# Sums of weights at a fixed place, more buffers, and block copies on another engine, in a hybrid decoder layer on one core

## Chip, cores and metric

The kernel runs on one core of a Trainium2 chip. The metric is the device time of one execution in microseconds (us). The engines are called TensorE (PE in the profile), VectorE (DVE), ScalarE (ACT), GpSimd (POOL) and SyncE (SP), which here issues nearly all transfers.

## What is computed

One decoder layer on 16 learned meta tokens and 1024 tokens of width 1024, all in float32: a SwiGLU FFN added at half weight, a token mixer added, a second FFN at half weight, a final norm.

```python
def swiglu(x, w_in, w_out):
    gate, up = jnp.split(x @ w_in, 2, axis=-1)
    return (jax.nn.silu(gate) * up) @ w_out

h = jnp.concatenate([meta, x], axis=1)
h = h + 0.5 * swiglu(rms_norm(h, ffn1_norm), ffn1_w_in, ffn1_w_out)
h = h + hybrid_mixer(rms_norm(h, mix_norm), ...)
h = h + 0.5 * swiglu(rms_norm(h, ffn2_norm), ffn2_w_in, ffn2_w_out)
return rms_norm(h, final_norm)[:, N_META:]
```

The mixer projects to 10256 columns and runs two branches of eight heads each: a gated DeltaNet (a causal convolution, then per chunk a triangular system and a scan over a 128x128 state) and a retention (rotary, a causal product with decay, a scan). Their outputs are gated, projected and added. The decay between two tokens of a chunk is used only where the second is not earlier than the first (the causal mask, `incl`).

## The kernel before

**Products.** Every float32 weight tile of 128x512 is loaded raw (`wraw`), cast on ScalarE to its rounded part (`wh`, `L136`) and split on GpSimd or VectorE into the rest (`wl`, `L137`); a product is three matmuls (`mm3`, `L158` to `L160`). `wraw`, `wh` and `wl` have four buffers each (`wtile`).

**The FFN** (`ffn`, called twice; tiles are named `start` in the first and `ffn` in the second) works on the 2816 hidden columns in 22 blocks `f` of 128. Each block makes Strassen-like combinations: `pair_weights` (`L220` to `L231`) takes four raw tiles (two of the gate, two of the up weights), adds and subtracts them in place on VectorE (`L223`, `L224`, `L226`, `L227`) and yields seven weight combinations in the order 0, 1, 2, 3, 5, 4, 6. `hidden` multiplies each with two groups of tokens; the list `order` has 14 entries `(i, grp)`. Products 0, 2, 4, 6 of a group grow in one PSUM bank (`mm`), 1 in a `px` bank and 3, 5 in another; between them ScalarE copies and VectorE's `add` (`L295`) reads the bank, so product 6 cannot start before the `add` that reads product 4. Gates are multiplied at `L298`; blocks with f % 4 of 0 or 1 also subtract at `L301`, those of 2 or 3 combine with the stored halves of block f - 2 in a tile `kept` (`L289` to `L312`). Finished operands go to DRAM (`opnd_d`).

After five groups of four blocks, `output` multiplies the operands with combinations of `w_out`. Those that need additions are made ahead in the hidden loop: at f = 4, 8, ..., 20 `load_sums` (`L378`) loads four 256 KB parts twice into tiles `sums`, and at f % 4 == 1, or at f = 20 for the last two, `weight_sums` (`L384`) does four VectorE additions of 128x512 (`L386` to `L389`) on each and stores 1 MB to `sums_d` (`L390`). The ten tiles per FFN, `kept`, the operand halves (`lower`, `upper`), `opnd`, `hh` and `hl` share the tag `hid` with two buffers.

**The mixer.** Retention runs first, a projection and a scan per head; after the projections of heads 1 to 4 `decays` makes the decay matrices of two DeltaNet heads each: a product on GpSimd (`L981`), a matmul, an exponential on ScalarE (`L986`), a store to `em_d`. Then `weave` interleaves the DeltaNet's chains with the remaining projections on TensorE, head by head. `gdn_systems` scales the key products by the decay into `X` (`L1125`), copies its 32x32 diagonal blocks to `Xc` on VectorE (`L1129`, four copies), goes through DRAM (`x_d`) for a substitution within blocks of 16 (`L1159`, `L1160`), doubles the inverses and copies blocks of 32 from `Uc` to `Ut` (`L1201`, four copies), then multiplies blocks (`tmp` at `L1213`, `L1218`). `gdn_scan` makes `Qk` (`L1287`), masks it with `incl` on GpSimd (`L1291`) and runs the state recurrence (`L1302` to `L1314`, state `st` at `L1312`).

**Order.** Each engine works through its own queue in order, SyncE's transfers too. The program's order is only a priority: the framework's planner runs a simulation of time (`schedule_with_timeline_sim`) and puts an instruction into its engine's queue when the simulated engine is free and its data and buffer are there. So an instruction can stand in a queue well ahead of its place in the program.

Of the kernel before, what the change touches and what calls it, by code (L numbers as in the profile page):

```python
# [10 lines left out]
F32 = mybir.dt.float32  # L11
F32R = mybir.dt.float32r
AF = mybir.ActivationFunctionType
ALU = mybir.AluOpType
PSUM = bass.MemoryType.PSUM

P = 128
# [79 lines left out]
def hybrid_layer(ctx, tc, a):  # L97
    nc = tc.nc
# [39 lines left out]
        return hi, lo  # L138

    def wtile(tag):  # L140
        return wp.tile([P, 4, P], F32 if tag == "wraw" else F32R, name=tag, tag=tag, bufs=4)

    def load_half(src):
        raw = wtile("wraw")
# [86 lines left out]
        yield 6, put_weights(rg[1], eng=V if 6 in fast else None)  # L231

    def operand_halves(fp, hn):
        return halves_of([fp.tile([P, 8 * hn], F32, name=n, tag="hid", bufs=2) for n in ("lower", "upper")])

    def halves_of(ts):
        return [t.rearrange("p (k h n) -> p k h n", k=4, h=2)[:, :, h] for h in range(2) for t in ts]
# [37 lines left out]
    def ffn(fp, hidp, hT, hn, slots, spare, second, w_in, w_out, last_blocks, last_weights, tail, first, w0=None):  # L275
# [6 lines left out]
        def hidden(f, ws, order, after):  # L282
            sg, q3, q1, q2 = (fp.tile([P, 2, hn], F32, name=n, tag="tmp", bufs=5) for n in ("sg", "q3", "q1", "q2"))
            chains = [[None, None], [None, None]]
            made = [0, 0]
            kept = None
            if f and f % 4 == 0:
                sums.extend(load_sums(f // 2 - 2 + e) for e in range(2))
            if f < 4 * ng and f % 4 > 1:  # L289
                kept = hidp.tile([P, 8 * hn], F32, name="kept", tag="hid", bufs=2).rearrange("p (u n) -> p u n", u=4)  # L290
                for u, i in enumerate((0, 4)):
                    SP.dma_start(kept[:, u], part_of(f - 2, i))

            def add(out, ps):
                V.tensor_tensor(out=out, in0=out, in1=ps, op=ALU.add)  # L295

            def gate(half, grp, x, g):
                V.tensor_tensor(out=x[:, grp], in0=x[:, grp], in1=g[:, grp], op=ALU.mult)  # L298
                made[half] += 1
                if half and f < 4 * ng and f % 4 < 2:  # L300
                    V.tensor_tensor(out=x[:, grp], in0=x[:, grp], in1=q3[:, grp], op=ALU.subtract)  # L301
                if made[half] == 2:
                    put_hidden(f, half, x)
                    if half and kept is not None:
                        flat = lambda t: t.rearrange("p g n -> p (g n)")
                        b11, t1, t2, d = (kept[:, u] for u in range(4))
                        V.tensor_tensor(out=t2, in0=flat(q2), in1=t1, op=ALU.subtract)
                        SP.dma_start(part_of(f, 2), t2)
                        G.tensor_tensor(out=b11, in0=t2, in1=b11, op=ALU.subtract)
                        SP.dma_start(part_of(f, 3), b11)  # L310
                        G.tensor_tensor(out=d, in0=flat(q3), in1=t2, op=ALU.subtract)
                        SP.dma_start(part_of(f, 5), d)  # L312

            for i, grp in order:
                if grp == 0 and sums and (f % 4 == 1 and i in (2, 5) or f == 4 * ng and i in (5, 6)):
                    weight_sums(*sums.pop(0))
                chain = i in (1, 3, 5)
                if i in (0, 1, 3):
                    chains[chain][grp] = psum(("mm", "px")[chain])[:, :hn]
                ps = chains[chain][grp]  # L320
                (wh, wl), (xh, xl) = ws[i], slots[grp][i]
                mm3(ps, [(wh[:, k], wl[:, k], xh[:, k], xl[:, k]) for k in range(4)], i in (0, 1, 3), i in (1, 5, 6), True)
                if i == 0:
                    S.copy(sg[:, grp], ps)
                elif i == 1:
                    add(sg[:, grp], ps)
                    S.activation(sg[:, grp], sg[:, grp], AF.Silu)
                elif i == 2:
                    S.copy(q3[:, grp], ps)
                elif i == 3:  # L330
                    S.copy(q2[:, grp], ps)
                elif i == 5:
                    add(q3[:, grp], ps)
                    gate(0, grp, q3, sg)
                elif i == 4:
                    add(q2[:, grp], ps)
                else:
                    S.activation(q1[:, grp], ps, AF.Silu)  # L338
                    gate(1, grp, q2, q1)
                if grp == 0:  # L340
                    after(i)
# [34 lines left out]
        sums = []  # L376

        def load_sums(n):  # L378
            w = hidp.tile([P, 8 * hn], F32, name="sums", tag="hid", bufs=2)[:, :16 * P].rearrange("p (i c) -> p i c", i=4)
            for i, (dh, fi) in enumerate(((0, 0), (0, 1), (1, 0), (1, 1))):  # L380
                SP.dma_start(w[:, i].rearrange("p (f c) -> p f c", f=2), block(4 * (n // 2), n % 2, fi, dh))
            return n, w

        def weight_sums(n, w):  # L384
            a11, a12, a21, a22 = (w[:, i] for i in range(4))
            V.tensor_tensor(out=a21, in0=a21, in1=a22, op=ALU.add)  # L386
            V.tensor_tensor(out=a11, in0=a21, in1=a11, op=ALU.subtract)
            V.tensor_tensor(out=a12, in0=a12, in1=a11, op=ALU.subtract)
            V.tensor_tensor(out=a22, in0=a22, in1=a11, op=ALU.subtract)  # L389
            SP.dma_start(sums_d[n], w.rearrange("p i c -> p (i c)"))  # L390

        LOADS = ((0, 1), (2, 3), (5, 4), (6,))

        def load_operands(g, pair):
            t = hidp.tile([P, 8 * hn], F32, name="opnd", tag="hid", bufs=2).rearrange("p (u k n) -> p u k n", u=2, k=4)
            for u, i in enumerate(pair):
                SP.dma_start(t[:, u].rearrange("p k n -> p (k n)"), opnd_d[7 * g + i])
            return t
# [65 lines left out]
            for _ in steps:  # L464
                pass
        f0 = 4 * ng
        hh, hl = (hidp.tile([P, 8 * hn], F32R, name=n, tag="hid", bufs=2) for n in ("hh", "hl"))
        for q in range(4):
            s = slice(2 * hn * q, 2 * hn * q + 2 * hn)
            raw = fp.tile([P, 2, hn], F32, name="raw", tag="tmp", bufs=5).rearrange("p a n -> p (a n)")  # L470
# [497 lines left out]
    def decays(hs):  # L968
# [9 lines left out]
        for h in hs:  # L978
            for gi, g in enumerate(GROUPS):
# [4 lines left out]
                ef = em.rearrange("p c d -> p (c d)")  # L984
                PE.matmul(pd, lhsT=strict, rhs=ef, start=True, stop=True)
                S.activation(ef, pd, AF.Exp)  # L986
                SP.dma_start(em_d[h][gi], ef)

    for h in range(H):
# [104 lines left out]
    def gdn_systems(h, kraw, vraw):  # L1094
# [31 lines left out]
                                       in1=ems[c // 4][:, c % 4], op0=ALU.mult, op1=ALU.mult)  # L1126
        for q in range(4):
            qs = slice(B2 * q, B2 * q + B2)
            V.tensor_copy(Xc[qs], X[qs, :, qs])  # L1129
        V.tensor_scalar(x16[:, :NCH], Xc[:, :, 0:BS], par[:, 0:1], None, op0=ALU.mult)  # L1130
        V.scalar_tensor_tensor(out=x16[:, :NCH], in0=Xc[:, :, BS:B2], scalar=par[:, 1:2], in1=x16[:, :NCH], op0=ALU.mult, op1=ALU.add)
        V.tensor_scalar(xoff[:, :, BS:B2], Xc[:, :, BS:B2], par[:, 0:1], None, op0=ALU.mult)
# [65 lines left out]
        tmp = bp.tile([P, CK * BS * BS * 3 // 4], F32, name="tmp", tag="xr", bufs=1)  # L1198
        for q in range(4):
            qs = slice(B2 * q, B2 * q + B2)  # L1200
            V.tensor_copy(Ut[qs, :, qs], Uc[qs])  # L1201

        At = tmp[:, :512].rearrange("p (c x) -> p c x", x=64)
        ps = psum("px")
# [40 lines left out]
    def gdn_scan(h, query, kf, vf, st, Ut, ems, rk, br, kd_s, v_s):  # L1245
# [33 lines left out]
        for j in range(0, NCH, 2):  # L1279
# [5 lines left out]
            for i in range(2):  # L1285
                c = j + i
                V.scalar_tensor_tensor(out=Qk[:, c], in0=ps[:, i * P:(i + 1) * P], scalar=rk[:, c + 1:c + 2],  # L1287
                                       in1=ems[c // 4][:, c % 4], op0=ALU.mult, op1=ALU.mult)
            if j % 4 == 2:
                qg = Qk[:, j - 2:j + 2]  # L1290
                G.tensor_tensor(out=qg, in0=qg, in1=incl.unsqueeze(1).broadcast_to([P, 4, P]), op=ALU.mult)  # L1291


        sso = sp.tile([P, CK], F32, name="sso")
# [259 lines left out]
```

## Time and profile before

| | us |
|---|---|
| median of 3 runs | 3125.59 |
| lowest and highest | 3121.34, 3128.95 |
| profiled execution | 3128.13 |
| its span, first to last instruction | 3126.2 |
| mean granted TensorE clock | 0.966 of full |

The profile comes from the profiled execution. A line of it names engine, kernel line, operation, the tile written and, behind the arrow, those read. A busy share is the time in which the engine executed; a wait names the engine and instruction that ended it. The granted clock is a share of 2.4 GHz and takes two levels, 2.4 and 1.2 GHz, so a mean of 0.93 is 14% of a stretch at the lower one. The stages in order: start and FFN1 to about 710 us, retention to 1316, DeltaNet with projections to 2090, branch outputs to 2400, FFN2 to the end.

### The profile page before, as it was taken

The numbers are of one execution on the slowest core, as the hardware profiler recorded it, in microseconds if no ns is written. First come the engines' busy times: TensorE is split into PE (matmuls) and PEld (weight loads), VectorE is DVE, ScalarE is ACT, GpSimd is POOL, SyncE is SP. The second block draws the span as 40 slices with busy tenths as digits, with TensorE's granted clock in tenths as the row PEclk, the third lists the DMA queues.
The fourth block names the chain that finished last, engine by engine and source line by source line (L and its number), as shares of the span: only waits on it lengthen the run. The fifth ranks groups of instructions, "written<-read, shape, count | busy, mean of one in ns | idle before, by whom it ended". The sixth has DMA issues, their size and how long they took to land. (4 is left out here: it accounts for less than half of the span.)

```text
span 3126.2 us, 55790 instructions
## 1 busy us (share of the span) xinstructions
PE 2942.6 (94%) x21463; PEld 2785.3 (89%) x21463; DVE 1836.4 (59%) x3363; ACT 1308.4 (42%) x2735; POOL 1662.2 (53%) x1419
## 2 busy tenths in 40 slices
PE   7999998999899999989999999999998999999998
PEld 6999998999789899988999898988888999998777
DVE  8544656886854655465556555562338554546765
ACT  5333334433554554444455445453234333334432
POOL 5545455663656656544555454545526555455752
PEclk8999999999899999989999899989999999999999
DMA  2444455642312121212221222153533444445742
GB/s 91 155 131 143 136 163 187 232 158 95 96 48 65 55 61 51 71 41 64 75 64 55 58 74 64 53 169 116 175 108 99 133 138 160 137 160 204 239 142 103
DMA packets 364412, 357.18 MB, mean 114 GB/s; under 512 B 29921, under 2 KB 294370, under 8 KB 361586
## 3 DMA queue, kind: packets, MB, share of 16 engines
q1 hardware_dynamic: 364080, 353.61, 36.2%
q8 instruction: 168, 2.75, 0.4%
q14 instruction: 98, 0.80, 0.1%
q10 hardware_dynamic: 66, 0.02, 0.0%
HBM read 263.24 MB, written 90.32 MB: 113 GB/s over the span
## 5 line engine op out<-in xcount | busy, mean ns | idle before, releaser
L137 POOL TENSOR_TENSOR wl<-wraw,wh 128x512 fp32r<-128x512 f32 x806 | 1106.0, 1379 | 1095.9 <-ACT wh L136 1037.1
L136 ACT CAST wh<-wraw 128x512 fp32r<-128x512 f32 x864 | 535.3, 622 | 1052.0 <-issue 177.8
L1022 DVE SCALAR_TENSOR_TENSOR cb<-raw,cw,cb 128x344 f32<-128x344 f32 (+2 forms) x216 | 137.2, 667 | 26.9 <-ACT cb L1020 25.6
L158 PE MATMUL ps_gate_mm<-act,wh 128*128 128x344 f32 (+1 forms) x352 | 122.9, 350 | 0.6 <-ACT raw L717 0.6
L158 PE MATMUL ps_ffn_mm<-on,wh 128*128 128x256 f32 (+1 forms) x376 | 110.3, 293 | 7.7 <-DVE q L295 5.9
L158 PE MATMUL ps_start_mm<-on,wh 128*128 128x260 f32 x392 | 112.3, 286 | 2.7 <-DVE q L295 2.4
L160 PE MATMUL ps_gate_mm<-act,wl 128*128 128x344 f32 (+1 forms) x352 | 114.5, 325 | 0.0
L159 PE MATMUL ps_gate_mm<-act,wh 128*128 128x344 f32 (+1 forms) x352 | 114.5, 325 | 0.0
L160 PE MATMUL ps_start_mm<-on,wl 128*128 128x260 f32 x392 | 111.6, 285 | 1.9 <-POOL wl L137 1.9
L159 PE MATMUL ps_start_mm<-on,wh 128*128 128x260 f32 x392 | 112.0, 286 | 0.0
L160 PE MATMUL ps_ffn_mm<-on,wl 128*128 128x256 f32 (+1 forms) x376 | 109.4, 291 | 0.2 <-POOL wl L137 0.2
L159 PE MATMUL ps_ffn_mm<-on,wh 128*128 128x256 f32 (+1 forms) x376 | 109.2, 290 | 0.0
L158 PE MATMUL ps_start_mm<-ox,wh 128*128 128x260 f32 x292 | 85.7, 294 | 18.8 <-DVE q L295 16.9
L158 PE MATMUL ps_start_px<-on,wh 128*128 128x260 f32 x308 | 88.4, 287 | 14.5 <-DVE q L295 12.5
L298 DVE TENSOR_TENSOR q<-q,q 128x260 f32<-128x260 f32 (+1 forms) x84 | 64.1, 763 | 59.5 <-ACT q L338 59.5
L158 PE MATMUL ps_ffn_mm<-ox,wh 128*128 128x256 f32 (+1 forms) x264 | 79.2, 300 | 17.1 <-DVE q L295 16.8
L159 PE MATMUL ps_start_px<-on,wh 128*128 128x260 f32 x308 | 88.1, 286 | 0.0
L159 PE MATMUL ps_start_mm<-ox,wh 128*128 128x260 f32 x292 | 84.7, 290 | 3.6 <-DVE ox L137 3.6
L160 PE MATMUL ps_start_px<-on,wl 128*128 128x260 f32 x308 | 88.0, 286 | 0.0
L160 PE MATMUL ps_start_mm<-ox,wl 128*128 128x260 f32 x292 | 85.0, 291 | 0.0
L160 PE MATMUL ps_ffn_px<-on,wl 128*128 128x256 f32 (+1 forms) x284 | 83.3, 293 | 0.8 <-POOL wl L137 0.8
L158 PE MATMUL ps_ffn_px<-on,wh 128*128 128x256 f32 (+1 forms) x284 | 83.5, 294 | 0.6 <-ACT wh L136 0.6
(1657 smaller groups left out, 10979.4 us busy)
## 6 DMA issues: line engine op xcount, KB each, us to landing
wraw<-ffn_w_in SPq DMA_DIRECT2D x176, 256.0 KB
wraw<-w_in SPq DMA_DIRECT2D x168, 256.0 KB
sums<-ffn_w_out SPq DMA_DIRECT2D x80, 256.0 KB
sums_d<-sums SPq DMA_DIRECT2D x20, 1024.0 KB
wraw<-sums_d SPq DMA_DIRECT2D x80, 256.0 KB
opnd<-opnd_d SPq DMA_DIRECT2D x35, 520.0 KB
opnd<-opnd_d SPq DMA_DIRECT2D x35, 512.0 KB
wraw<-ffn_w_out SPq DMA_DIRECT2D x68, 256.0 KB
```

The costliest lines, as they stand in the source:

```text
L136: S.copy(hi, raw)
L137: (eng or G).tensor_tensor(out=lo, in0=raw, in1=hi.bitcast(F32), op=ALU.subtract)
L158: PE.matmul(ps, lhsT=wh, rhs=xh, start=first and i == 0, stop=False, skip_group_check=grow)
L159: PE.matmul(ps, lhsT=wh, rhs=xl, start=False, stop=False, skip_group_check=grow)
L160: PE.matmul(ps, lhsT=wl, rhs=xh, start=False, stop=last and i == n - 1, skip_group_check=grow)
L298: V.tensor_tensor(out=x[:, grp], in0=x[:, grp], in1=g[:, grp], op=ALU.mult)
L1022: V.scalar_tensor_tensor(out=c, in0=raw[:, s0 + k:s0 + k + n], scalar=cw[:, 24 * k + ct:24 * k + ct + 1], in1=c, op0=ALU.mult, op1=ALU.add)
```

## The change

- The four additions of a `sums` tile become a generator, one per step, each pinned: `keep_in_program_order` puts an instruction behind the one that was traced before it on its engine (order of issue only, no wait for its end). In blocks f % 4 == 1 one step is taken before each product from the fifth entry of `order` on, at f = 20 from the sixth; after four steps the store follows and the next tile begins.
- `wraw` gets six buffers, the tag `hid` three. Their room comes from the SBUF that is set aside for descriptors of transfers issued by software, which is cut to 256 bytes per partition.
- The copies to `Xc` and to `Ut` (four each per head) move from VectorE to ScalarE.
- The decay matrices are masked with `incl` once, in `decays`, between the exponential and the store; the mask on `Qk` in `gdn_scan` goes.

```diff
-        return wp.tile([P, 4, P], F32 if tag == "wraw" else F32R, name=tag, tag=tag, bufs=4)
+        return wp.tile([P, 4, P], F32 if tag == "wraw" else F32R, name=tag, tag=tag, bufs=6 if tag == "wraw" else 4)
...
-        return halves_of([fp.tile([P, 8 * hn], F32, name=n, tag="hid", bufs=2) for n in ("lower", "upper")])
+        return halves_of([fp.tile([P, 8 * hn], F32, name=n, tag="hid", bufs=3) for n in ("lower", "upper")])
...
-                sums.extend(load_sums(f // 2 - 2 + e) for e in range(2))
+                sums.extend(weight_sums(*load_sums(f // 2 - 2 + e)) for e in range(2))
...
-            for i, grp in order:
-                if grp == 0 and sums and (f % 4 == 1 and i in (2, 5) or f == 4 * ng and i in (5, 6)):
-                    weight_sums(*sums.pop(0))
+            for at, (i, grp) in enumerate(order):
+                if f % 4 == 1 and at > 3 or f == 4 * ng and at > 4:
+                    while sums and next(sums[0], sums) is sums:
+                        sums.pop(0)
...
         def weight_sums(n, w):
             a11, a12, a21, a22 = (w[:, i] for i in range(4))
-            V.tensor_tensor(out=a21, in0=a21, in1=a22, op=ALU.add)
-            V.tensor_tensor(out=a11, in0=a21, in1=a11, op=ALU.subtract)
-            V.tensor_tensor(out=a12, in0=a12, in1=a11, op=ALU.subtract)
-            V.tensor_tensor(out=a22, in0=a22, in1=a11, op=ALU.subtract)
+            for out, x, y, op in ((a21, a21, a22, ALU.add), (a11, a21, a11, ALU.subtract), (a12, a12, a11, ALU.subtract), (a22, a22, a11, ALU.subtract)):
+                tc.keep_in_program_order(V.tensor_tensor(out=out, in0=x, in1=y, op=op))
+                yield
             SP.dma_start(sums_d[n], w.rearrange("p i c -> p (i c)"))
...
                 S.activation(ef, pd, AF.Exp)
+                G.tensor_tensor(out=em, in0=em, in1=incl.unsqueeze(1).broadcast_to([P, 4, P]), op=ALU.mult)
                 SP.dma_start(em_d[h][gi], ef)
...
-            V.tensor_copy(Xc[qs], X[qs, :, qs])
+            S.copy(Xc[qs], X[qs, :, qs])
...
-            V.tensor_copy(Ut[qs, :, qs], Uc[qs])
+            S.copy(Ut[qs, :, qs], Uc[qs])
...
-            if j % 4 == 2:
-                qg = Qk[:, j - 2:j + 2]
-                G.tensor_tensor(out=qg, in0=qg, in1=incl.unsqueeze(1).broadcast_to([P, 4, P]), op=ALU.mult)
...
-    nc = bacc.Bacc("TRN2", target_bir_lowering=False, num_devices=1)
+    nc = bacc.Bacc("TRN2", target_bir_lowering=False, num_devices=1, dynamic_dma_scratch_size=256)
```

The other places with the tag `hid` (`kept`, `sums`, `opnd`, `hh`, `hl`) change from two to three buffers in the same way.

## Rows read from the trace of the kernel before

**Rows 1.** Page, part 1: busy us, share of the span and instructions by engine.

```profile
PE 2942.6 (94%) x21463; PEld 2785.3 (89%) x21463; DVE 1836.4 (59%) x3363; ACT 1308.4 (42%) x2735; POOL 1662.2 (53%) x1419
```

**Rows 2.** Waits of TensorE, whole run: us in total, times, longest.

```profile
PE ps_ffn_mm L158 <- DVE q L295: 22.7, 10, 3.4
PE ps_start_mm L158 <- DVE q L295: 19.2, 6, 3.7
PE ps_start_px L158 <- DVE q L295: 12.5, 4, 4.1
```

**Rows 3.** Stretches: length, busy us of PE, PEld, DVE, ACT, POOL; clock, DMA share, GB/s.

```profile
116.40:526.80 410.40, 379.99 (x3048) 377.82 (x3047) 214.85 (x318) 137.19 (x307) 200.38 (x147) 0.97 0.49 157
116.40:167.10 50.70, 44.54 (x344) 44.12 (x343) 27.57 (x40) 15.15 (x35) 25.72 (x19) 0.93 0.56 182
167.10:206.80 39.70, 39.70 (x333) 39.70 (x332) 19.48 (x32) 15.37 (x34) 18.54 (x15) 1.00 0.34 102
2470.10:2866.80 396.70, 374.86 (x3047) 373.04 (x3046) 200.34 (x318) 138.31 (x307) 201.40 (x147) 0.97 0.49 161
2470.10:2518.00 47.90, 43.34 (x342) 42.93 (x341) 25.82 (x41) 15.18 (x34) 24.69 (x18) 0.93 0.57 193
2518.00:2557.60 39.60, 39.60 (x334) 39.60 (x334) 17.39 (x30) 15.49 (x36) 19.38 (x15) 1.00 0.32 101
```

**Rows 4.** VectorE in order of time, 126 to 136: start, us, instruction, [idle before].

```profile
126.58 0.42 DVE L295 TENSOR_TENSOR q<-q,ps_start_px 128x260 f32<-128x260 f32 x1 [6.50 <-PE ps_start_px L160]
130.45 0.69 DVE L386 TENSOR_TENSOR sums<-sums 128x512 f32<-128x512 f32 x1 [3.45 <-DMA wraw<-ffn_w_in]
...
133.68 0.41 DVE L295 TENSOR_TENSOR q<-q,ps_start_mm 128x260 f32<-128x260 f32 x1
```

**Rows 5.** SyncE's queue in order of time, 117 to 156.

```profile
122.80 0.90 SPq L381 DMA_DIRECT2D sums<-ffn_w_out  x2
...
152.63 0.32 SPq L390 DMA_DIRECT2D sums_d<-sums  x1
153.00 1.50 SPq L145 DMA_DIRECT2D wraw<-ffn_w_in  x2
```

**Rows 6.** VectorE in order of time, 152 to 162.

```profile
159.48 0.69 DVE L223 TENSOR_TENSOR wraw<-wraw 128x512 f32<-128x512 f32 x1 [5.11 <-DMA wraw<-ffn_w_in]
160.09 0.42 DVE L295 TENSOR_TENSOR q<-q,ps_start_px 128x260 f32<-128x260 f32 x1
```

**Rows 7.** Tile sums, whole run: duration ns min/median/max, first and last start.

```profile
L389 DVE TENSOR_TENSOR sums<-sums x20: 678/1227/1783, 135.2 to 2852.9; 128x512 f32<-128x512 f32 x20
```

**Rows 8.** VectorE in order of time, 167 to 188, a block without sums beside it.

```profile
176.62 0.43 DVE L295 TENSOR_TENSOR q<-q,ps_start_px 128x260 f32<-128x260 f32 x1 [6.06 <-PE ps_start_px L160]
...
178.58 0.69 DVE L223 TENSOR_TENSOR wraw<-wraw 128x512 f32<-128x512 f32 x1 [1.08 <-DMA wraw<-ffn_w_in]
...
182.03 0.41 DVE L295 TENSOR_TENSOR q<-q,ps_start_mm 128x260 f32<-128x260 f32 x1
```

**Rows 9.** TensorE in order of time, 182.4 to 183.

```profile
182.58 0.31 PE L158 MATMUL ps_start_mm<-on,wh 128*128 128x260 f32 x1
```

**Rows 10.** Lines 1129 and 1213, whole run: duration ns min/median/max.

```profile
L1129 DVE COPY Xc<-X x32: 281/284/1418, 1348.7 to 2040.7; 32x256 f32<-32x256 f32 x32
...
L1213 ACT COPY tmp<-ps_g0sys_px x1: 363/363/363, 1394.9 to 1394.9; 32x256 f32<-32x256 f32 x1
```

**Rows 11.** The DeltaNet stretch, columns as in rows 3.

```profile
1316.00:2090.00 774.00, 729.31 (x6188) 694.57 (x6186) 454.89 (x1066) 372.93 (x872) 387.15 (x392) 0.95 0.24 66
```

**Rows 12.** Waits of TensorE in the mixer: us in total, times, longest.

```profile
PE ps_g5scan_gx L1302 <- DVE st L1312: 5.3, 1, 5.3
...
PE ps_r4proj_mm L160 <- POOL wl L137: 2.2, 2, 1.1
...
PE ps_g4sys_px L1218 <- DVE tmp L1213: 0.9, 1, 0.9
```

**Rows 13.** Line 1291, whole run: duration ns min/median/max.

```profile
L1291 POOL TENSOR_TENSOR Qk<-Qk,masks x16: 1277/1306/1748, 1426.1 to 2127.4; 128x512 f32<-128x512 f32 x16
```

More of the change, by code (lines that the diff above doesn't have):

```diff
@@ L287, in hidden @@
             if f and f % 4 == 0:
-                sums.extend(load_sums(f // 2 - 2 + e) for e in range(2))
+                sums.extend(weight_sums(*load_sums(f // 2 - 2 + e)) for e in range(2))
             if f < 4 * ng and f % 4 > 1:
-                kept = hidp.tile([P, 8 * hn], F32, name="kept", tag="hid", bufs=2).rearrange("p (u n) -> p u n", u=4)
+                kept = hidp.tile([P, 8 * hn], F32, name="kept", tag="hid", bufs=3).rearrange("p (u n) -> p u n", u=4)
                 for u, i in enumerate((0, 4)):
@@ L378, in load_sums @@
         def load_sums(n):
-            w = hidp.tile([P, 8 * hn], F32, name="sums", tag="hid", bufs=2)[:, :16 * P].rearrange("p (i c) -> p i c", i=4)
+            w = hidp.tile([P, 8 * hn], F32, name="sums", tag="hid", bufs=3)[:, :16 * P].rearrange("p (i c) -> p i c", i=4)
             for i, (dh, fi) in enumerate(((0, 0), (0, 1), (1, 0), (1, 1))):
@@ L394, in load_operands @@
         def load_operands(g, pair):
-            t = hidp.tile([P, 8 * hn], F32, name="opnd", tag="hid", bufs=2).rearrange("p (u k n) -> p u k n", u=2, k=4)
+            t = hidp.tile([P, 8 * hn], F32, name="opnd", tag="hid", bufs=3).rearrange("p (u k n) -> p u k n", u=2, k=4)
             for u, i in enumerate(pair):
@@ L466, in ffn @@
         f0 = 4 * ng
-        hh, hl = (hidp.tile([P, 8 * hn], F32R, name=n, tag="hid", bufs=2) for n in ("hh", "hl"))
+        hh, hl = (hidp.tile([P, 8 * hn], F32R, name=n, tag="hid", bufs=3) for n in ("hh", "hl"))
         for q in range(4):
```

## Prediction

> **What bounds the kernel now.** I read the engine shares first: TensorE is busy 94% of the span, VectorE 59%, ScalarE 42%, GpSimd 53% [rows 1]. So a change is worth what it takes from TensorE's idle time or from the time at its lower clock, and nothing else. The list of TensorE's waits comes next: its three longest entries are one and the same wait, a matmul of an FFN behind VectorE's `add` (`L295`), 54.4 us in 20 waits of up to 4.1 us [rows 2]. Where these lie is seen by cutting the hidden loop at its first `sg` copies into pairs of blocks `f`: with `load_sums` work beside it a pair takes 50.7 us (FFN1) or 47.9 us (FFN2) at a granted clock of 0.93, without it 39.7 or 39.6 us at 100% busy and 1.00 [rows 3]. From f = 3 to 20 each FFN has nine pairs, five with sums. Had all nine the clean length, FFN1 would take 9 x 39.7 = 357.3 us for 410.4, FFN2 9 x 39.6 = 356.4 for 396.7: **53.1 + 40.3 = 93.4 us** hang on the ten groups of sums. What the same rows show as idle or as lost clock is a little less: 410.4 - 380.0 = 30.4 us idle and 3% of clock (12.3 us), in FFN2 21.8 and 11.9, together 76.4 us. The remaining 17 us are gaps that modelled matmul ends hide; I take 76 and 93 as the two ends of what there is to win.
>
> The timelines then show two kinds of stall. First kind: VectorE comes to the first sum (`L386`) at 127.0 and waits for a transfer until 130.45; behind it in VectorE's order stand a gate product, a weight sum and the group's second addition, and only then, at 133.68, the `add` that TensorE needs [rows 4]. The loads of these sums went out from 122.80 [rows 5], after the buffer of `kept` had come free, and the sum stands in block 3, though the program has it in block 5: the planner moved it up, to where in its own time the data was there. Second kind: SyncE stands at the store of the sums (`L390`) until 152.63 and issues two weight loads behind it at 153.00 [rows 5]; VectorE reaches `L223` with nothing to add, waits 5.11 us until 159.48, and the `add` follows at 160.09 [rows 6].
>
> **The change part by part. FFN.** The third `hid` buffer lets the first sums load while two `kept` tiles are alive, the second when one of them goes, both one to two blocks ahead (20 us each) of their use. The pin holds each addition behind the VectorE instruction traced before it, so none can stand in block 3 or 4 any more. That removes the first kind. For the second: with four raw buffers a block's last weight load waits for the last release of the block before; with six it waits for the release two weights earlier, 2/7 of a block or some 5.7 us, more than the 5.11 us of the wait. What is late next is the added work at its new place. Each sum is one VectorE addition of 128x512: 678 ns at its shortest, 1227 median, 1783 longest [rows 7]. Of a group's eight, five (steps 4 to 8) come where the trace of an undisturbed block has VectorE idle for 6.06 us, until 176.62 [rows 8]: 5 x 1.23 = 6.1 us, so they just fit. Three stand between the gate products; there TensorE takes up the last product at 182.58 and the `add` that it needs runs from 182.03 to 182.44 [rows 8, 9], 0.14 us of slack. Two of them lie ahead of that `add`: 2 x 0.68 to 2 x 1.23 = 1.4 to 2.5 us more; against that `L223` with its wait (1.08 + 0.69 us, [rows 8]) moves into the idle time, 1.8 us less. Net -0.4 to +0.7 us; I take the 0.7 and half a microsecond for a window that is only just long enough, 1.2 us per group, 12 us for ten, and as bounds 0 and, if every addition takes nearly its longest, what the first rival says. **FFN: -93.4 + 12 = -81 us.** The buffers themselves cost nothing on an engine; the 20 stores and 80 loads of sums are as many as before.
>
> **DeltaNet copies.** 64 copies of 32x256 leave VectorE, 284 ns each by the median of those to `Xc` [rows 10]: about 18 us over 774 us in which VectorE is busy 59% [rows 11]. On ScalarE such a copy takes 363 ns [rows 10], 23 us, where it is busy 48%. Both lie beside TensorE's work. What TensorE can gain directly is its wait for the block product `tmp` behind the `Ut` copies, 0.9 us in head 4 [rows 12] and as much or less in two others, some 2 us; the upper bound is its wait for the scan state, 5.3 us in head 5 [rows 12], 18 us over all heads, which has other VectorE work ahead of it as well. The lower bound is the slower rival below. I take **-2 us**.
>
> The Trainium skill speaks against this part: Perfetto Trace Analysis, section Optimizing Scalar/DVE Operations, has VectorE faster where it has a performance mode, and offloading as sensible if VectorE is saturated. The rows agree on the first (284 against 363 ns), and 59% is not saturated; by the page this part brings nothing, 2 us less gain.
>
> **The mask.** 16 GpSimd products of 128x512 (1.3 us each, [rows 13]) leave the scan and 16 come between exponential and store in `decays`. In the scan no matmul waited for them in the trace. In the retention stage TensorE already waits for GpSimd's weight split, 2.2 us in head 4 [rows 12], just in the heads that run `decays`; four more products there can add some tenths each: 0 to 10 us, the top if each of the 16 delays a split by half its 1.3 us. SyncE's store behind them waits about 1.3 us longer, with weight loads queued behind it, which two spare raw buffers cover; without that cover it is those same 1.3 us for each. I take **+2 us**.
>
> **The sum.** The profiled execution took 3128.1 us: 3128 - 81 - 2 + 2 = 3047. It lies 2.5 us above the median of the runs (3125.6), so **3045**. The forecast's own range: 3015 (no residue, and all 18 us of scan waits gone) to 3062 (76 us to win instead of 93).
>
> **The rivals.** *Sums against splits.* The additions stretch from 0.68 to 1.78 us [rows 7]; the long ones ran while GpSimd's splits ran without a break. If all take 1.7 us, five overrun the window by 5 x 1.7 - 6.06 = 2.4 us and two more cost 3.4, less the 1.8 of `L223` and 0.1 of slack: 3.9 us of stall, with a clock drop of the size of today's (12.3 + 11.9 us for ten groups, 2.4 each) some 6.3 us a group, 63 us in all. Gain 93 - 63 = 30: 3096. For it: GpSimd is busy 18.5 of a clean pair's 39.7 us [rows 3]. Against: that is under half, and such a block has no `kept` work. The Trainium skill states the mechanism (SBUF — State Buffer, section Who interferes with whom): a VectorE instruction with two SBUF inputs and a GpSimd one that reads SBUF exclude each other; the stretch in the trace agrees.
>
> *Only the first kind goes.* If the weight loads stay behind the sums' store, the second stalls stay: the four waits on the `px` bank in FFN1, 12.5 us, and in FFN2 what is left of 22.7 us without five of 3.4, 5.7 us [rows 2]. Scaled by 93.4 to 54.4, for clock and hidden gaps, that is 31 us. Gain 93 - 31 - 12 = 50: 3076. Against it: a lead of two buffers is longer than the wait.
>
> *Slower.* In DeltaNet, ScalarE's four copies wait for `X` and for `Uc`, and behind them in its order stand `vn`, the projections' evacuations and the weight casts. If the planner takes `X` for earlier than the chip has it, each of 16 places (two per head) stops TensorE, as one late VectorE instruction does now for up to 5.3 us [rows 12], with some 2.5 us of clock. 16 x 7.8 = 125 us: 3045 + 125 = 3170. From 5 us a place on it eats the whole gain. Against: the same copies stand in VectorE's order today, under the same wait, ahead of as urgent work.
>
> *Nothing moves.* The additions land where they did in effect, or new stalls as long take over: 3126.
>
> **How the numbers follow.** Forecast 0.62, sums against splits 0.14, only the first kind 0.14, slower 0.05, nothing 0.05. A measurement of this kernel tells 0.2% (6 us) from no change. Faster is the first three, 0.90; same 0.04 (most of the last); slower 0.06. The range leaves out the last two cases and a tail at either end: 3015 to 3100.
>
> **What would show it.** Right: pairs of blocks with sums at 40 to 42 us and a granted clock near 1.00; the first `L386`-like addition in block 5 with no transfer ahead of it; no `L223` wait of 5 us; the three `L295` waits of TensorE together under 15 us. Wrong: waits of the last product behind the additions in block 5 (first rival); `L223` still waiting (second); TensorE waiting for ScalarE copies between 1316 and 2090 us (slower). I would be wrong altogether if the new plan lengthens stages that the change doesn't touch.

## The result, and the profile after

| | before | after |
|---|---|---|
| median, us | 3125.97 (4 runs) | 3055.66 (4 runs) |
| lowest and highest, us | 3121.34, 3128.95 | 3054.29, 3058.65 |
| after over before | | 0.9778, 95% interval 0.9761 to 0.9795 |
| span of the profiled execution, us | 3126.2 | 3052.6 |
| mean granted clock | 0.966 | 0.977 |

The kernel became 2.2% faster: 70.3 us between the medians and 73.6 us between the two profiled spans, where the prediction had 81. First the stretches from block 3 to block 21 of either FFN, and the first two pairs of blocks in FFN1, in the kernel after; they answer to [rows 3] and have its columns.

```profile
117.50:485.20 367.70, 365.67 (x3038) 364.69 (x3037) 217.74 (x319) 140.23 (x309) 201.19 (x149) 1.00 0.53 170
117.50:157.80 40.30, 40.30 (x338) 40.30 (x337) 19.55 (x32) 15.39 (x35) 23.58 (x19) 1.00 0.48 153
157.80:198.20 40.40, 40.40 (x338) 40.31 (x337) 27.27 (x40) 15.38 (x34) 19.68 (x15) 1.00 0.55 177
2427.90:2791.70 363.80, 361.78 (x3039) 361.37 (x3039) 213.71 (x319) 139.17 (x310) 203.97 (x149) 1.00 0.53 171
```

FFN1 went from 410.4 to 367.7, FFN2 from 396.7 to 363.8, together **75.6 us less**. TensorE is busy for all but 2 us of each stretch, at full clock, and the pair with the sums' additions is as long as the one without (40.4 against 40.3). Everything outside the two stretches adds up to 2.0 us more; the stretches hold 18 matmuls fewer than before (3038 and 3039 against 3048 and 3047), about 2.2 us at 0.12 us each, which accounts for these 2.0 us. The first group's sums now stand in block 5, mostly in VectorE's idle time. VectorE in order of time, 146 to 176, after; this answers to [rows 4], [rows 6] and [rows 8]:

```profile
146.39 0.91 DVE L223 TENSOR_TENSOR wraw<-wraw 128x512 f32<-128x512 f32 x1 [5.12 <-DMA wraw<-ffn_w_in]
147.77 0.43 DVE L295 TENSOR_TENSOR q<-q,ps_start_px 128x260 f32<-128x260 f32 x1 [0.47 <-PE ps_start_px L160]
...
161.34 4.89 DVE L388 TENSOR_TENSOR sums<-sums 128x512 f32<-128x512 f32 x5
166.15 1.78 DVE L223 TENSOR_TENSOR wraw<-wraw 128x512 f32<-128x512 f32 x1
167.92 0.42 DVE L295 TENSOR_TENSOR q<-q,ps_start_px 128x260 f32<-128x260 f32 x1
...
173.33 1.78 DVE L388 TENSOR_TENSOR sums<-sums 128x512 f32<-128x512 f32 x1
```

Five additions run without a gap and no transfer stands ahead of them. `L223` still waits 5.12 us for its weight at 146.39, but the `add` behind it (147.77) is itself still waiting for TensorE: a wait as long as the one of [rows 6] now costs nothing.

### The profile page after: what moved, and what is told of

Read it like the earlier page. It is cut to its first block, busy times and chain, and to the rows that moved or that the text cites. A ratio compares the mean times of both kernels' runs of the same rounds, so it can differ in the third digit from the quotient of the medians.

```text
span 3052.6 us, 55749 instructions
## 1 busy us (share of the span) xinstructions
PE 2905.5 (95%) x21463; PEld 2754.0 (90%) x21463; DVE 1806.9 (59%) x3299; ACT 1333.5 (44%) x2797; POOL 1651.6 (54%) x1419
## 5 line engine op out<-in xcount | busy, mean ns | idle before, releaser
L223 DVE TENSOR_TENSOR wraw<-wraw 128x512 f32<-128x512 f32 x42 | 51.5, 1226 | 163.7 <-DMA wraw<-ffn_w_in 157.1
L1023 DVE SCALAR_TENSOR_TENSOR cb<-raw,cw,cb 128x344 f32<-128x344 f32 (+2 forms) x216 | 130.7, 637 | 25.7 <-ACT cb L1021 24.0
L388 DVE TENSOR_TENSOR sums<-sums 128x512 f32<-128x512 f32 x80 | 83.8, 1067 | 0.7
```

Source lines behind the costliest of these rows:

```text
L223: V.tensor_tensor(out=ru[0], in0=ru[0], in1=ru[1], op=ALU.add)
L388: tc.keep_in_program_order(V.tensor_tensor(out=out, in0=x, in1=y, op=op))
L1023: V.scalar_tensor_tensor(out=c, in0=raw[:, s0 + k:s0 + k + n], scalar=cw[:, 24 * k + ct:24 * k + ct + 1], in1=c, op0=ALU.mult, op1=ALU.add)
```

## Experiments

Runs of one batch share runs of the kernel before; across batches I compare ratios. Every time below is a median, with its ratio to the kernel before and the 95% interval. "Stretches" are block 3 to block 21 of FFN1 and FFN2 in the profile.

### Which part brings it: the FFN part alone, the mixer part alone

Two kernels: the first has pins, six raw and three `hid` buffers with the old mixer; the second has only the copies on ScalarE and the mask in `decays`, with the one on `Qk` gone. The second's edit in part:

```diff
-            V.tensor_copy(Xc[qs], X[qs, :, qs])
+            S.copy(Xc[qs], X[qs, :, qs])
...
+                G.tensor_tensor(out=em, in0=em, in1=incl.unsqueeze(1).broadcast_to([P, 4, P]), op=ALU.mult)
```

> The FFN part alone: pinned sums, six raw buffers, three hid buffers; copies and mask as before. My theory (the whole gain is the FFN's, the mixer's parts cancel): 3056 us, within 5 of the full change; blocks 3 to 20 take 368 us in FFN1 and 364 us in FFN2 (before 410.4 and 396.7), and the stretch between them is as before, 1943 us. Rival (the mixer's parts matter, a loss in retention and a gain in DeltaNet that differ): over 3062 or under 3050.

> The mixer part alone: copies on ScalarE and the mask in the decays; FFN and buffers as before. My theory: 3126 us, within 6 of before. Rival (it brings its own gain): under 3118. Slower rival of the prediction (ScalarE's queue stops TensorE): over 3132, with TensorE waiting for ScalarE instructions between 1316 and 2090 us.

FFN part: 3055.87 us, 0.9772 [0.9758, 0.9786], stretches 367.2 and 363.2. Mixer part: 3127.05 us, 1.0003 [0.9992, 1.0014]. The whole gain is the FFN's. The mixer's zero is a sum of two shifts, taken up below.

### Buffers alone, pins alone

> The buffers alone (six raw, three hid), sums not pinned. My theory (buffers remove the late weight loads, the pin removes the sums that stand too early): the first kind of stall stays, some 3.4 us of wait with its clock per group, the second goes; gain about 31 us, 3095. Rival (a third hid buffer brings the sums early enough wherever they stand): all goes, 3056. Rival (only the pin does anything): 3126.

> The pin and the spreading alone, four raw and two hid buffers. My theory: the first kind of stall goes, the second stays, since weight loads still stand behind the store of the sums: gain about 50 us, 3076, VectorE waiting at its weight sum in block 5 or 6 and TensorE behind it. Rival (the place of the sums is all that counts): 3056. Rival (without the buffers the sums come too late for their fixed place): above 3090, VectorE waiting for sums in block 5.

Buffers: 3076.48 us, 0.9839 [0.9824, 0.9854], stretches 374.3 and 374.5. Pins: 3106.68 us, 0.9929 [0.9916, 0.9943], stretches 395.1 and 403.2. My theory had the order wrong: the pins were to bring the larger part and brought 20 us, the buffers 51. The time lies where the last rival had it, above 3090, but not for its reason: VectorE waits for sums only twice in the whole run, 6.4 us in all. What the pins leave is a wait for weights. It is seen in SyncE's queue and on VectorE, 148 to 157, with the pins alone, and then in TensorE's waits in FFN1's stretch:

```profile
148.14 1.92 SPq L382 DMA_DIRECT2D sums<-ffn_w_out  x4
150.11 1.02 SPq L145 DMA_DIRECT2D wraw<-ffn_w_in  x2
```

```profile
156.40 0.69 DVE L223 TENSOR_TENSOR wraw<-wraw 128x512 f32<-128x512 f32 x1 [5.50 <-DMA wraw<-ffn_w_in]
157.01 0.42 DVE L295 TENSOR_TENSOR q<-q,ps_start_mm 128x260 f32<-128x260 f32 x1
```

```profile
PE ps_start_mm L158 <- DVE q L295: 17.5, 12, 3.3
```

The weights go out behind the *loads* of a sums tile, not only behind a store as in [rows 5]; `L223` is free to run at 150.9, waits until 156.40, and the `add` that TensorE needs comes behind it. TensorE's stop ahead of that product is 3.3 us (from 154.23).

### Which buffers: six raw with two operand buffers, four raw with three

Both have pins and the old mixer. The lines that change, in part and against the kernel after, for the first and for the second:

```diff
-... tag="hid", bufs=3 ...
+... tag="hid", bufs=2 ...
```

```diff
-... bufs=6 if tag == "wraw" else 4)
+... bufs=4)
```

> Sums pinned and spread and six raw weight buffers, but two operand buffers as before; the mixer as before. Together with the pins alone (3106.7), with all of the FFN part (3055.9) and with three operand buffers on four raw ones it fills the table of pins with {4, 6} raw by {2, 3} operand buffers. Theory: what the pins alone left is weight loads that come late behind the sums' transfers in SyncE's queue, and the raw buffers let them be issued two loads sooner; so six raw buffers carry nearly all of the 50.8 us that the buffers bring: 3055 to 3066 us, and the stretch from block 3 to block 21 366 to 372 us in each FFN (with pins alone 395.1 and 403.2). Rival: the third operand buffer carries it, because kept, operand and sums tiles wait for each other's release and hold SyncE's queue up: then this run stays at 3095 to 3107 us, with stalls of 2 to 3 us ahead of TensorE in blocks 3 to 5 of each group.

> Sums pinned and spread and three operand buffers, but four raw weight buffers as before; the mixer as before. Theory (the raw buffers carry the buffers' gain): 3095 to 3107 us, the stretches near 395 and 403 us, the waits of the weight sums for weight loads still 80 us or more together. Rival (the operand buffer carries it): 3056 to 3066 us. If the two are needed together, both this run and the one with six raw and two operand buffers end above 3080 us.

Six raw and two `hid`: **3038.50 us, 0.9731 [0.9713, 0.9749]**, stretches 368.3 and 364.0, about as short as with three:

```profile
117.70:486.00 368.30, 365.80 (x3031) 365.23 (x3030) 219.79 (x319) 140.68 (x310) 201.16 (x149) 1.00 0.53 172
2422.00:2786.00 364.00, 361.66 (x3028) 361.45 (x3027) 214.56 (x319) 139.45 (x309) 202.26 (x148) 1.00 0.53 173
```

Four raw and three `hid`: 3104.53 us, 0.9943 [0.9925, 0.9961], stretches 389.6 and 396.2. With the pins in place the raw buffers carry the gain, as the theory had it, and the first of these kernels is also faster than the changed one, which no theory had. It saves behind block 21. TensorE's longest waits there in FFN2 (2791.7 to the end with three buffers, 2786 to the end with two), first the changed kernel, then the one with two:

```profile
PE ps_ffn_gx L158 <- DVE hm L440: 9.4, 3, 5.1
PE ps_ffn_mm L158 <- ACT q L339: 1.6, 1, 1.6
```

```profile
PE ps_ffn_mm L158 <- DVE hm L440: 3.1, 2, 1.7
```

`L440` adds the output products into the hidden state and frees the bank that the next product takes. With a third buffer the operands of the products behind block 21 are loaded sooner. In the run with the FFN part alone the first two loads go out at 2771.68 and the next two at 2780.77, block 21 begins at 2787.0; with two buffers the first two go out at 2778.00 and the next from 2787.41, block 21 begins at 2786.0:

```profile
2780.77 0.80 SPq L397 DMA_DIRECT2D opnd<-opnd_d  x2
```

```profile
2787.41 3.65 SPq L397 DMA_DIRECT2D opnd<-opnd_d  x4
```

Their splits stand otherwise in VectorE's queue, in the order that the planner makes: in the first of these runs TensorE stands from 2817.3 to 2822.4 for two additions of `L440` that come behind a pair of splits:

```profile
2818.17 3.45 DVE L137 TENSOR_TENSOR on<-opnd,on 128x512 fp32r<-128x512 f32 x2
2821.54 1.28 DVE L440 SCALAR_TENSOR_TENSOR hm<-ps_ffn_gx,hm 128x512 f32<-128x512 f32 x2
```

Early loads alone do not bring this. The kernel with the doubled additions (below) also has three buffers and loads as early, at 2797.88 and 2809.80 with block 21 at 2816.4; there TensorE waits for this line (`L442` in that kernel) only once in FFN2, and the rest takes 255.8 us, as with two buffers (255.5) and not as in the run with the FFN part alone (261.5):

```profile
PE ps_ffn_gx L158 <- DVE hm L442: 2.3, 1, 2.3
```

So the third buffer's price lies in the order that the planner came to with it; what leads it there was not tested. From block 3 to the end of the FFN the price is 4 us in FFN1 and 5 us in FFN2 by the spans; the ratios differ by 0.0041, 13 us, with an uncertainty of some 7.

### How much lead a weight load needs, and what the raw buffers do without the pins

```diff
-bufs=6 if tag == "wraw" else 4
+bufs=5 if tag == "wraw" else 4
```

The second kernel is the kernel before with six raw buffers and nothing else.

> Sums pinned and spread, five raw weight buffers, two operand buffers, the mixer as before: one raw buffer between the run with four (3106.7 us) and that with six (3038.5 us). Theory of the prediction, by the lead: a further buffer lets a weight load go out one weight earlier, 1/7 of a block or 2.9 us, and the waits were 3.8 to 5.5 us, so one buffer covers half to three quarters of them and a wait of 1 to 2.6 us is left: 3055 to 3075 us. Rival (the lead does not scale like that: the store of the sums, with SyncE behind it, decides, and one free buffer is enough): 3037 to 3045 us.

> Six raw weight buffers alone: the sums as before (neither pinned nor spread), two operand buffers, the mixer as before. Theory: with three operand buffers and no pins the stretches were 374.3 and 374.5 us and the time 3076.5; the third operand buffer costs 10 to 12 us behind block 21 and brings the unpinned sums little, so 3062 to 3070 us, and the pins are worth 25 to 30 us of the rest. Rival: without the pins the sums need the third buffer, since their loads can only go out when a kept tile goes, and VectorE then waits for them among the gate products as before: 3080 to 3095 us, with waits of 3 us and more for the load of the sums ahead of TensorE's add.

Five raw buffers with pins: 3085.27 us, 0.9870 [0.9849, 0.9891], stretches 389.2 and 387.7. Six raw without pins: 3084.21 us, 0.9874 [0.9858, 0.9889], stretches 398.0 and 383.8. Both missed what the theory gave them and were slower. With five, loads of sums still get between a block's weight loads; SyncE's queue and VectorE, 207 to 218 (TensorE stands for 3.30 us there, from 216.80):

```profile
207.55 1.44 SPq L145 DMA_DIRECT2D wraw<-ffn_w_in  x1
210.97 0.90 SPq L382 DMA_DIRECT2D sums<-ffn_w_out  x2
211.97 0.41 SPq L145 DMA_DIRECT2D wraw<-ffn_w_in  x1
212.42 1.02 SPq L382 DMA_DIRECT2D sums<-ffn_w_out  x2
213.49 0.47 SPq L145 DMA_DIRECT2D wraw<-ffn_w_in  x1
```

```profile
216.91 1.40 DVE L223 TENSOR_TENSOR wraw<-wraw 128x512 f32<-128x512 f32 x1 [10.82 <-DMA wraw<-ffn_w_in]
```

So the lead does not scale by one seventh of a block per buffer, as I had it. Without the pins the first kind stays, the rival's prediction for that run: VectorE in FFN1, block 3, with TensorE standing for 4.41 us from 130.64:

```profile
128.74 0.69 DVE L386 TENSOR_TENSOR sums<-sums 128x512 f32<-128x512 f32 x1 [3.02 <-DMA wraw<-ffn_w_in]
```

The table that these runs fill (ratio to the kernel before; stretches in us; all with the old mixer):

| pins | raw | hid | ratio | FFN1 | FFN2 | sum |
|---|---|---|---|---|---|---|
| no | 4 | 2 | 1 | 410.4 | 396.7 | 807.1 |
| yes | 4 | 2 | 0.9929 | 395.1 | 403.2 | 798.3 |
| yes | 4 | 3 | 0.9943 | 389.6 | 396.2 | 785.8 |
| no | 6 | 2 | 0.9874 | 398.0 | 383.8 | 781.8 |
| yes | 5 | 2 | 0.9870 | 389.2 | 387.7 | 776.9 |
| no | 6 | 3 | 0.9839 | 374.3 | 374.5 | 748.8 |
| yes | 6 | 3 | 0.9772 | 367.2 | 363.2 | 730.4 |
| yes | 6 | 2 | 0.9731 | 368.3 | 364.0 | 732.3 |

With two `hid` buffers the pins alone bring 8.8 us, six raw buffers alone 25.3, both together 74.8: **40.7 us come only when both are there.** The first group of four blocks shows why; the same 674 matmuls, first with pins alone, then with six raw buffers alone, then the changed kernel (before it is 50.7 + 39.7 = 90.4, [rows 3]):

```profile
117.50:205.40 87.90, 82.74 (x674) 82.33 (x674) 44.43 (x71) 30.53 (x69) 42.24 (x33) 0.98 0.47 151
```

```profile
116.00:202.80 86.80, 82.39 (x674) 82.19 (x674) 44.99 (x71) 30.76 (x69) 42.91 (x33) 0.98 0.48 153
```

```profile
117.50:198.20 80.70, 80.70 (x674) 80.61 (x673) 46.81 (x71) 30.77 (x68) 43.26 (x33) 1.00 0.52 165
```

Late weights alone cost 7.2 us here, the early sums alone 6.1, both together 9.7, not 13.3. My reading, which no run tested by itself: while TensorE stands for one of them, the other's transfer gets on.

### How full the window of block 5 is

Each pinned addition is done twice, first into a spare tile.

```diff
+                tc.keep_in_program_order(V.tensor_tensor(out=spare_sum[0], in0=x, in1=y, op=op))
                 tc.keep_in_program_order(V.tensor_tensor(out=out, in0=x, in1=y, op=op))
```

> The changed kernel with each of the pinned additions of sums done twice (first into a spare tile): eight more additions of 128x512 in each of the ten groups, some 8 us of VectorE each at the 0.98 us that five took in 4.89. It asks how much room is left where the additions stand. Theory: the five in the idle window of block 5 and the weight sum behind them end just as TensorE needs the add, so nearly all of the added time of the window, 4 to 5 us, becomes a stall, with the two among the gate products 1 to 2 us more: 40 to 65 us in all, 3096 to 3121 us. Rival: there is room, since the weight sum waits there for its load in blocks without sums: under 1 us a group, 3056 to 3066 us.

3079.08 us, 0.9854 [0.9836, 0.9872]: 24 us above the changed kernel, below what the theory had and far above its rival. The stretches are 385.4 and 380.6, 34.5 us more for ten groups; some 8.5 us of this come back behind block 21 (245.8 and 255.8 us against 249.2 and 260.9) and some 5 in the mixer (1309.8 against 1315.0), which the edit leaves alone. In the first block with sums TensorE stops once, for 2.51 us from 172.01, behind VectorE's `add`; from 174.2 on the granted clock is at its lower level, in the columns of [rows 3]:

```profile
174.20:177.60 3.40, 3.08 (x14) 3.08 (x15) 3.40 (x6) 0.11 (x2) 1.27 (x1) 0.50 0.05 22
```

Half the clock (1.2 GHz) over 3.4 us is 1.7 us more, so this 2.5 us stop costs 4.2 by my estimate; the group is 4.1 us longer (84.8 against 80.7). Over the first group of four blocks:

```profile
117.30:202.10 84.80, 82.29 (x674) 82.08 (x674) 53.23 (x79) 30.67 (x68) 42.59 (x33) 0.98 0.49 157
```

VectorE is busy 6.4 us longer than in the changed kernel's group (46.81 there), and TensorE stops for 2.5: about 4 us of the added work found room.

### The last group one step earlier

```diff
-                if f % 4 == 1 and at > 3 or f == 4 * ng and at > 4:
+                if (f % 4 == 1 or f == 4 * ng) and at > 3:
```

> The changed kernel with the last group's additions (block 20) started at the same place as those of the other groups, one step earlier (at > 3 in place of at > 4). Theory: the last block is 23.4 to 23.5 us long where a block with sums is 20.0 to 20.9, because two additions follow each other ahead of a weight sum and TensorE waits 1.6 us twice for it; one step earlier there is a window of VectorE to take one of them. Gain 2 to 3.4 us per FFN, so 3049 to 3052 us. Rival: the two additions that the last group places late stand there because the block has fewer steps of the first half left, and starting earlier moves the stall to an earlier step: 3055 to 3057 us.

3051.21 us, 0.9778 [0.9754, 0.9802]: by the ratio no different from the changed kernel, but with an uncertainty of some 9 us this cannot tell the 2 to 3.4 us per FFN of the theory from the nothing of the rival. The stretches say more: they are 0.9 us shorter each, less than the theory had. The stall did not move to an earlier step either, as the rival had it: the stop of 1.6 us in block 20 is gone and no gap above 0.5 us is left. Yet the block still measures 23.0 us, for it holds 183 matmuls between its marks where a usual one holds 171, and 22.24 us of busy time against 20.20. So 2.0 of the 3.4 us that I had read as a loss were other work inside the cut.

### Mask and copies apart, and the best of all

The first is the changed kernel with the mask back in `gdn_scan`; the second has two `hid` buffers beside that.

> The changed kernel with the mask back in the scan's place (a multiplication on GpSimd behind every four products) and out of the decays; the block copies stay on ScalarE. In the changed kernel the retention stage is 8.4 us longer than before and the DeltaNet stage 11.8 us shorter. Theory: the longer retention is the mask's, which GpSimd now does among the work of the heads that come with decays, and the shorter DeltaNet is the copies': then the retention stage goes back to 482 us and the DeltaNet stage stays near 733, and the time is 3046 to 3050 us. Rival: both are the mask's (it left the scan and went to the decays): the retention stage goes back to 482, the DeltaNet stage to 742 to 744, and the time is 3054 to 3058 us.

> The changed kernel with two operand buffers in place of three and with the mask back in the scan: sums pinned, six raw weight buffers and the copies on ScalarE stay. The run with six raw and two operand buffers took 3038.5 us with the mixer as before; its stretches from block 3 to 21 were as short as with three (368.3 and 364.0 us), and what follows block 21 was shorter by 5 us in either FFN. Theory: the third operand buffer costs these 10 to 12 us, and the copies without the mask bring 5 to 8 us beside that, since they are in another stage: 3029 to 3035 us. Rival: the copies' gain was only another order of the mixer that the planner happened on, and with another plan it is gone: 3038 to 3045 us.

Without the mask in `decays`: 3050.27 us, 0.9768 [0.9748, 0.9787]; by its ratio no different from the changed kernel, and so no decision between theory and rival. The stages tell more than the time. The end of retention (projection of head 5 to the first DeltaNet gate) takes 176.2 us in the changed kernel and 163.9 here. Four kernels with the mask in `decays` have 172.4 to 176.7, the others all 163.8 to 163.9. TensorE's waits in it, changed kernel:

```profile
PE ps_r4scan_px L958 <- DVE rog L957: 2.2, 3, 1.2
PE ps_r6proj_mm L158 <- ACT rv L705: 1.8, 1, 1.8
PE ps_r6proj_mm L158 <- DVE rv L649: 1.7, 1, 1.7
```

and the granted clock behind the last of them:

```profile
1164.20:1171.00 6.80, 5.43 (x18) 5.43 (x19) 3.10 (x5) 1.85 (x4) 4.06 (x4) 0.50 0.28 73
```

The last masking multiplication starts at 1082.9, 80 us before the two waits of head 6, so it does not stand in their way itself; that the plan which it brought does is inferred. Against that the projection of head 1 to that of head 5 is shorter with the mask (237.7 to 239.3 us against 240.4 to 243.2). But my mark moved here: between the first matmuls of these two projections 1454 start with the mask and 1466 without, and in the end of retention 1090 and 1078. On equal work, from the projection of head 1 to the first gate, the changed kernel and the one without the mask:

```profile
826.50:1240.60 414.10, 397.31 (x2548) 377.97 (x2545) 211.97 (x459) 206.63 (x395) 268.37 (x260) 0.98 0.20 56
```

```profile
825.30:1230.50 405.20, 391.05 (x2548) 372.39 (x2545) 223.95 (x459) 208.16 (x397) 246.13 (x244) 1.00 0.20 57
```

The four kernels with the mask in `decays` take 411.7 to 414.4 us here, the others 404.3 to 407.0: some 7 us. The copies show in the DeltaNet, heads 4 to 7: 299.2 to 302.2 us in all six kernels with copies on ScalarE, 309.2 to 313.3 in those without. The same matmuls in the changed kernel and in the one with the FFN part alone (which has the old mask too):

```profile
1647.50:1949.40 301.90, 285.95 (x2457) 273.99 (x2456) 161.01 (x388) 158.25 (x375) 143.73 (x151) 0.97 0.23 63
```

```profile
1635.40:1947.80 312.40, 293.34 (x2457) 281.22 (x2456) 175.31 (x412) 148.31 (x351) 151.81 (x157) 0.95 0.22 61
```

From the first gate to head 4, however, the two kernels with the copies alone take 411.9 and 413.2 us, the eight with neither 404.6 to 412.0. Over the whole mixer up to the branch outputs the means are 1316.9 us with neither (eight kernels, 1314.7 to 1318.7), 1311.8 with the copies alone (two, 1310.8 and 1312.7), 1314.7 with both (four, spread 1309.8 to 1322.2): copies about -5, mask about +3, the latter inside its spread.

The best: **3037.97 us, 0.9717 [0.9703, 0.9732]**, stretches 368.3 and 364.2, clearly faster than both kernels. Against the run with six raw and two `hid` buffers on the old mixer (0.9731 [0.9713, 0.9749]) the copies' gain cannot be told from nothing; the expectation (3029 to 3035) was too good.

## Why the prediction held, and which steps of it did not

**What to win.** The 93.4 us were mis-sized, and [rows 3] could have shown it: the clean pair of 39.7 us has 333 matmuls, the pair before it 344, while the two pairs of after shown above have 338 each and take 40.3 and 40.4 us. The stalled block had shifted the `sg` copy by which I cut, so some matmuls of the clean pair were counted with its neighbour. At TensorE's busy time after, 365.7 + 361.8 = 727.5 us, there were 807.1 - 727.5 = 79.6 to win, some 2 less on equal work. The other end that I had worked out, idle time and lost clock, 76.4 us, was the right one; I had put the 17 us between them down to gaps that modelled ends hide, and they were not there.

**The residue.** 12 us were allowed for additions that overrun; by 79.6 to win and 75.6 won it is 4.0, of which the two stops in block 20 are 3.2 (1.59 and 1.65). Only the last pair of each FFN, which holds block 20, is outside the 40 to 42 us that I named (43.7 and 43.4). I had priced five additions in the window at 1.23 us each, they took 4.89 together. That 1.23 was the median of one of the four lines [rows 7]; over all 80 additions the median was 1.05 before, and it is 0.69 now:

```profile
L388 DVE TENSOR_TENSOR sums<-sums x80: 677/692/1793, 161.3 to 2785.9; 128x512 f32<-128x512 f32 x80
```

So the two errors, 14 us too much to win and 8 too much residue, partly cancel: -81 forecast, -75.6 found. That the forecast of 3045 came within 11 us of the median is in part this luck. Of the 11 us, some 6 are these two terms, 2 the rest of the span, and the others the place of the profiled execution among its runs (2.5 us above the median before, 1.4 below it after).

**The two kinds of stall.** Both exist, and the change removes both, but their weights were wrong. I gave the second kind 31 us by the places where TensorE stood [rows 2]. With pins alone, the kernel of that rival, the stretches are 66.0 us longer than with six raw buffers beside them (798.3 against 732.3), and the time is 3106.7, not 3076. Alone the second kind costs these 66.0 us and the first 49.5 (781.8 against 732.3), the two together 74.8: they overlap, and the share by where TensorE stood, 31 and 62, missed that. The cause was also named too narrowly: not only the store [rows 5] but the loads of the sums hold the weight loads back. The argument by the lead (5.7 us against a wait of 5.11) gave the right answer for six buffers and failed for five. Even with six the waits did not go where it said: VectorE's waits at `L223` for a weight grew from 58.5 to 157.1 us in all, in 29 places before and after, but TensorE hardly stands behind them any more.

**The third `hid` buffer.** I had it as part of the cure of the first kind. It is one without the pins (six raw: 781.8 to 748.8 us), but beside pins and six raw buffers it brings 1.9 us in the stretches and costs 11 behind block 21 (5.1 and 6.0), 9 in all. "The buffers themselves cost nothing on an engine" was the failed step: with the third buffer the planner ordered VectorE's work otherwise, and splits stood ahead of `L440`.

**Copies.** Forecast -2, found about -5 in the mixer, from two kernels; the times of whole kernels cannot tell it from nothing. It is more than the direct wait for `tmp`, which is gone, and within the upper bound of the scan waits [rows 12]. In heads 4 to 7 most of it is not waiting but TensorE's busy time, 286.0 against 293.3 us for the same matmuls, at a granted clock of 0.97 against 0.95. They take more on ScalarE than the 0.36 us of [rows 10]:

```profile
L1130 ACT COPY Xc<-X x32: 400/403/407, 1316.0 to 1998.8; 32x256 f32<-32x256 f32 x32
```

and heads 4 to 7 are some 10 us shorter even so. The Trainium skill's Perfetto Trace Analysis, section Optimizing Scalar/DVE Operations, has offloading as sensible if VectorE is saturated. Here VectorE was busy 59% [rows 1] and that stage still became shorter, which speaks against the reading that the copies bring nothing; a gain in the time of a whole kernel is not shown.

**Mask.** Forecast +2, found about +3 with a spread of more than its own size: some 7 us more in retention, given back in part in the DeltaNet. I had priced it by delayed splits; what shows in retention are waits of head 6 for VectorE and ScalarE and a lower clock behind them.

**The rivals.** Sums against splits did not happen, but what it feared of an overrun window is real: the doubled additions bring the late `add`, the stop and the lower clock that it described. The long additions have not gone: 24 of 80 still take over 1.6 us, 31 before. The Trainium skill's SBUF — State Buffer, section Who interferes with whom, states that a VectorE instruction with two SBUF inputs contends with a GpSimd instruction that reads SBUF. The trace agrees: in the changed kernel GpSimd is at work for at least two thirds of each addition over 1.6 us, and for 30% on average of those under 0.8. None of TensorE's waits in the DeltaNet is put down to the copies; VectorE waits 8.0 us for those to `Xc`, in six places. Of what was to show the forecast right, pairs of 40 to 42 us (all but the last), clock 1.00 and the first sum in block 5 came; "no `L223` wait of 5 us" did not, harmlessly; the waits of [rows 2], 54.4 us, are down to 2.2 us, the two `q` lines here (the `sg` line had 3.2 us before):

```profile
PE ps_start_px L158 <- DVE sg L295: 3.0, 2, 1.9
PE ps_start_mm L158 <- DVE q L295: 1.8, 2, 1.5
PE ps_ffn_mm L158 <- DVE q L295: 0.4, 1, 0.4
```

**Open.** Which decision of the plan brings the waits of head 6 in retention was not tried; nor was the mask in `decays` without the copies. The pin and the spreading of the additions over the block were always changed together, so what each of them brings is not known.

## What to carry to other kernels

Cut a trace by equal work, not by a mark that a stall can shift: compare the matmul counts of the pieces before taking their difference as a gain. Two stalls that overlap hide each other, so price a partial cure by removing one at a time, and expect little from either alone. Give a buffer first to the tile that is late: where an instruction order is planned from buffer releases, a spare buffer elsewhere can change that order and put work in the way of something urgent.

## What the runs showed that I had not expected

- A fifth raw buffer brought 21.4 us in the stretches with pins and two `hid` buffers (798.3 to 776.9), the sixth another 44.6 (to 732.3): no diminishing return up to there. More than six was not tried.
- More on-chip memory made a kernel slower: three `hid` buffers 3055.87 us (0.9772), two 3038.50 (0.9731), all else equal.
- A stop of 2.51 us was followed by 3.4 us at half clock, in the kernel with doubled additions; the stop of 1.6 us in block 20 of the changed kernel was followed by none.
